# Attention written in pairs of beats: transposes of one, scores and projections of both, sums of one, transposes and sums of the other

## The chip, the cores and the metric

The kernel runs on one core of a Trainium2 chip. The metric is the device time of one execution in microseconds, from repeated runs; the changed kernel is compared with this one on the same chip. One execution was profiled; all rows here are from it.

## What is computed

One inference step of a trunk of two layers on 1024 latent tokens (a request in progress) and 256 context tokens, width 1024. The first layer mixes with two recurrences (mLSTM and SSD), the second with two attentions; each is followed by a squared-ReLU MLP, with RMSNorm and modulation around it. The change lies in the second layer's attentions:

```python
def odd_mixer_lat(h, k_ctx, v_ctx, ckv_ctx, kpe_ctx, cos_c, sin_c, cos_d, sin_d,
                  w_in, sink, q_a_norm, kv_a_norm, w_q_b, w_kv_b, w_out):
    ...
    oc = banded_attention(qc.reshape(Bsz, T, NKV_C, G_C, HD_C), kc, vc, k_ctx, v_ctx,
                          sink.reshape(NKV_C, G_C), HD_C ** -0.5)
    ...
    k, v = mla_keys_values(jnp.concatenate([ckv_ctx, ckv], axis=1),
                           jnp.concatenate([kpe_ctx, kpe], axis=1), w_kv_b)
    od = blocked_attention(qd[:, :, :, None], k, v, None, MLA_SCALE)
    return jnp.concatenate([oc.reshape(Bsz, T, -1), od.reshape(Bsz, T, -1)], axis=-1) @ w_out
```

`banded_attention` is grouped attention: 8 query heads, 2 key heads of 64, a band of 128 keys to either side, 256 context keys and a sink logit. `blocked_attention` on latent keys has 8 heads of 96 with all 1280 keys. The context tokens go through the same two without band, with 256 keys. All is in float32, and the kernel carries most products as three products of high and low parts.

## The kernel before

`Odd.run` issues the second layer's first projections, then the two attentions, and meanwhile the projections that the latent attention needs. All attention is cut into items that go through `weave` (line 2031):

- `Gqa` (line 1809): one tile of 128 queries and one key head with its four query heads; 10 tiles by 2, 20 items. Tiles 1 to 6 have five blocks of keys, three near and two of context; tiles 0 and 7 have four, and the context tokens' tiles 8 and 9 two.
- `Mla` (line 1919): two tiles of 128 latent queries and one head; 8 heads by 4, 32 items, five blocks of 256 keys each. The context tokens' share of a head is not an item; `Mla.alone` gives it in three steps.

The work goes in beats `n`. Every five beats an item starts, and its age `d` is the number of beats since. By age an item does this:

- `scores` at d = 0 to 4: products of queries and keys into PSUM. k = 0 and 1 fill the first score buffer (tag `S`, two buffers), k = 3 and 4 the second, k = 2 a third tile (tag `S3`, one buffer: `S3` in `Gqa`, `SB` in `Mla`). `Gqa` adds the band's mask by products with `idb`.
- `peak` at 1, 2 and 4: maxima on VectorE; `exps` at 3 to 6: exponentials on ScalarE from PSUM to SBUF (`Pm`, `Pmm`), with the sum in a second record, ACTIVATION_READ_ACCUMULATOR. In `Mla` exps at 3 and 5 read 1024 columns of `SA`, at 4 and 6 256 of `SB`; in `Gqa` each reads 512 of `S` and 128 of `S3`.
- `flip` at 7 and on, one for each block: four transposes of 128x128 by TensorE into a PSUM tile (`ptp`, `ptm`; tag `tp`, two buffers). `keep` in the same beat copies it to SBUF (`PT`, `PTm`), on VectorE at d = 9 and 11, on ScalarE else.
- `mix` one beat later: the product of block and values, summed in one PSUM bank (`po`, `pom`; tag `po`, one buffer). Values have 64 columns, so two such products stand in two halves of the array.
- `close` with the last mix, d = 12 with five blocks: the row sums' reciprocals (`R`, `Rm`, spread by POOL) are turned by products with the identity, ScalarE copies the sum, VectorE multiplies, and the bank is free again.

After the items' own work a beat calls `fill(n)`, which in beats 1, 2 and 4 of five takes one step of the extra projections: in the grouped stage the rest of the query projection (`qaps`, 8 pieces), the latent values (`vps`, 12), the queries' rotated parts (`qrps`, 10); in the latent stage `Mla.alone` (with scores `SC`, 8 times), and the next head's `qnps` (12), `knps` (24) and `qrtp` (transposes). Each lands in a tile with tag `tp` and is evicted by ScalarE and VectorE.

TensorE, ScalarE and VectorE run all of this in the order written:

```python
IN_ORDER = {mybir.EngineType.PE, mybir.EngineType.Activation, mybir.EngineType.DVE}
...
                with self.tc.manual_schedule(engines=IN_ORDER):
                    weave(nc, items(), fill)
```

A new tile in a buffer waits until the old tile's last reader is done; that is the only thing that holds an engine besides its data.

Of the kernel before, what the change touches and what calls it, by code (L numbers as in the profile page):

```python
# [75 lines left out]
KEEP = ((9,11),(9,11))  # L76
# [1732 lines left out]
class Gqa:  # L1809
# [31 lines left out]
    def scores(self, k):  # L1841
        if k == 2:
            if self.third:
                self.S3 = self.pp.tile([P, 4, P], F32, tag="S3", name="S3", bufs=1)
                for j in range(4):
                    self.product(self.S3[:, j], j, self.third[0], 1)
            return
        h = k - k // 3
        p, j = h // 2, h % 2
        if j == 0:  # L1850
            self.S[p] = self.pp.tile([P, 2, 512], F32, tag="S", name="S", bufs=2)
        for o, c0, nb in self.runs:
            self.product(self.S[p][:, j, o:o + nb * P], h, c0, nb)
# [176 lines left out]

def weave(nc, items, fill):

    act, dve = nc.scalar.copy, nc.vector.tensor_copy
    live, n = [], 0
    items = iter(items)
    while True:
        if n % 5 == 0:
            it = next(items, None)
            if it is not None:
                live.append((n, it))  # L2040
        live = [(b, x) for b, x in live if n - b <= 12]
        if not live:
            break
        at = [(n - b, x) for b, x in live]
        for d, x in at:
            if 0 <= d - 7 < x.tiles:
                x.flip(d - 7)
        for d, x in at:
            if d < 5:
                x.scores(d)  # L2050
        for d, x in at:
            if 0 <= d - 7 < x.tiles:
                x.keep(d - 7, dve if d in KEEP[0 if x.tiles < 5 or isinstance(x, Gqa) else 1] else act)
        for d, x in at:
            if d == SUMS:
                x.sums()
        for d, x in at:
            if d in (1, 2, 4):
                x.peak(d)
        for d, x in at:  # L2060
            if 3 <= d < 7:
                x.exps(d - 3)
        for d, x in at:
            if 0 <= d - 8 < x.tiles:
                x.mix(d - 8)
            if d - 8 == x.tiles - 1:
                x.close()
        fill(n)
        n += 1


KV_ORDER = (0, 1, 2, 3, 8, 9, 4, 5, 6, 7)
# [2 lines left out]
class Odd:  # L2075
# [332 lines left out]
    def run(self, late):  # L2408
        nc, net, a = self.nc, self.net, self.a
        pool = net.pool  # L2410
        with pool("od", 1) as cp:
# [113 lines left out]
            with pool("om", 4) as self.Pm, pool("oa") as sp, pool("oap", psum=True) as pp:  # L2525
# [41 lines left out]
                with self.tc.manual_schedule(engines=IN_ORDER):  # L2567
                    weave(nc, items(), fill)
                    while rest:
                        advance()  # L2570
# [54 lines left out]
```

## Time and profile before

| what | value |
| --- | --- |
| median of 3 runs | 3383.02 us (3382.25 to 3388.16) |
| the profiled execution | 3388.01 us, span of its instructions 3386.2 us |
| TensorE busy | 3233.2 us, 95% of the span |
| VectorE, ScalarE, POOL busy | 2250.5, 1634.0, 535.9 us |
| mean granted clock of TensorE | 0.980 |

The span runs from the first to the last instruction; the time has about 1.8 us more around it. A busy share is the union of the records of an engine. TensorE's matmuls are pipelined, and the end of a record is modelled: what two matmuls cost is the distance of their starts. The attention items run from about 1874 to 2457 us of the span.

### The profile page before, as it was taken

How to read it: one execution, taken by the hardware profiler on the slowest of the kernel's cores; microseconds unless marked ns; L12 is line 12 of the kernel's file. 1: busy time of each engine (PE TensorE's matmuls, PEld its weight loads, DVE VectorE, ACT ScalarE, POOL GpSimd, SP SyncE). 2: the span in 40 equal slices, each digit the busy share in tenths (PEclk: the TensorE clock that was granted, in tenths of full speed). 3: DMA queues.
4: the chain of work that ended last, by engine and by line, in shares of the span. 5: the costliest groups of instructions: out<-in, count | busy, mean ns of one | idle time of the engine just before them, and what ended most of it. 6: DMA issues, size and time to landing. Idle time of an engine off the chain costs nothing. (4 is left out here: it accounts for less than half of the span.)

```text
span 3386.2 us, 49959 instructions
## 1 busy us (share of the span) xinstructions
PE 3233.2 (95%) x17957; PEld 2644.1 (78%) x17957; DVE 2250.5 (66%) x4196; ACT 1634.0 (48%) x3827; POOL 535.9 (16%) x949
## 2 busy tenths in 40 slices
PE   7899999979999999999989999999999999999998
PEld 4898788858888888888787776666688788888887
DVE  4665866664598987788664466666746866556666
ACT  4444544453544444434563556555645444444443
POOL 1112222221111111001220240000011111110112
PEclk8999999979999999999999999999999999999999
DMA  7244343364355556565522210000233543365444
GB/s 216 71 110 116 104 140 102 81 203 142 115 171 179 182 181 227 181 204 159 160 95 90 72 40 26 9 5 7 83 132 108 175 143 142 119 208 171 156 142 174
DMA packets 319333, 435.26 MB, mean 129 GB/s; under 512 B 29772, under 2 KB 210348, under 8 KB 319084
## 3 DMA queue, kind: packets, MB, share of 16 engines
q1 hardware_dynamic: 296492, 343.17, 33.0%
q0 software_dynamic: 22592, 88.89, 7.0%
q8 instruction: 141, 2.31, 0.3%
q14 instruction: 108, 0.88, 0.1%
HBM read 309.55 MB, written 122.43 MB: 128 GB/s over the span
## 5 line engine op out<-in xcount | busy, mean ns | idle before, releaser
L194 PE MATMUL y<-oph 128*128 128x512 f32 x896 | 348.7, 389 | 1.7 <-DVE y L726 1.7
L196 PE MATMUL y<-oph,opl 128*128 128x512 f32 x896 | 348.6, 389 | 0.0
L195 PE MATMUL y<-opl,oph 128*128 128x512 f32 x896 | 348.6, 389 | 0.0
L200 DVE TENSOR_TENSOR opl<-sa,oph 128x512 fp32r<-128x512 f32 x216 | 158.9, 735 | 169.1 <-ACT oph L199 168.8
L199 ACT CAST oph<-sa 128x512 fp32r<-128x512 f32 x216 | 133.9, 620 | 263.9 <-PE y L195 180.2
L194 PEld LDWEIGHTS y<-oph 128*128 128x128 f32 x896 | 168.2, 188 | 37.1 <-DVE y L726 2.1
L195 PEld LDWEIGHTS y<-opl,oph 128*128 128x128 f32 x896 | 168.2, 188 | 35.1
L196 PEld LDWEIGHTS y<-oph,opl 128*128 128x128 f32 x896 | 168.2, 188 | 34.9
L480 POOL DMA_DIRECT2D hd<-x x96 | 52.0, 542 | 650.6 <-ACT x L482 507.0
L194 PE MATMUL mmf<-hh,wf_hi 128*128 128x512 f32 (+1 forms) x384 | 152.4, 397 | 0.0
L194 PE MATMUL mmt<-wt_hi,hh 128*128 128x256 f32 x480 | 148.0, 308 | 0.0
L196 PE MATMUL mmf<-hh,wf_lo 128*128 128x512 f32 (+1 forms) x384 | 139.3, 363 | 0.0
L195 PE MATMUL mmf<-hl,wf_hi 128*128 128x512 f32 (+1 forms) x384 | 138.9, 362 | 0.0
L195 PE MATMUL mmt<-wt_lo,hh 128*128 128x256 f32 x480 | 136.1, 283 | 0.0
L196 PE MATMUL mmt<-wt_hi,hl 128*128 128x256 f32 x480 | 136.0, 283 | 0.0
L1073 DVE SCALAR_TENSOR_TENSOR u<-pre,cw,u 128x510 f32<-128x510 f32 (+2 forms) x192 | 127.9, 677 | 7.2 <-ACT u L1071 6.3
L194 PE MATMUL o<-wh,hh 128*128 128x512 f32 x280 | 113.0, 404 | 0.0
L406 ACT ACTIVATE x<-x 128x512 f32<-128x512 f32 x112 | 70.2, 629 | 86.3 <-DVE x L640 65.7
L205 POOL TENSOR_SCALAR rs_v<-ss 128x1 f32<-128x1 f32 x85 | 30.5, 359 | 508.0 <-ACT junk L964 342.7
L196 PE MATMUL o<-wh,hl 128*128 128x512 f32 x280 | 110.5, 395 | 0.0
L195 PE MATMUL o<-wl,hh 128*128 128x512 f32 x280 | 110.1, 393 | 0.0
L2001 PE MATMUL pom<-PTm,mla_h 128*64 128x256 f32 x336 | 106.5, 402 | 2.4 <-DVE ob L2013 1.7
(1076 smaller groups left out, 10186.5 us busy)
## 6 DMA issues: line engine op xcount, KB each, us to landing
sa<-hd SPq DMA_DIRECT2D x108, 512.0 KB
hd<-s POOLq DMA_DIRECT2D x128, 320.0 KB, 3.0
hd<-x POOLq DMA_DIRECT2D x96, 320.0 KB, 2.6
wh<-in_w_down SPq DMA_DIRECT2D x40, 512.0 KB
wl<-in_w_down SPq DMA_DIRECT2D x40, 512.0 KB
w_raw<-in_w_ada SPq DMA_DIRECT2D x32, 512.0 KB
wh<-in_w_up SPq DMA_DIRECT2D x30, 512.0 KB
wl<-in_w_up SPq DMA_DIRECT2D x30, 512.0 KB
```

Source lines behind the costliest of these rows:

```text
L194: mm(ps, lh, rh, start=first and j == 0, stop=False)
L195: mm(ps, lh, rl, start=False, stop=False)
L196: mm(ps, ll, rh, start=False, stop=last and j == n - 1)
L199: self.nc.scalar.copy(hi, raw)
L200: self.nc.vector.tensor_tensor(lo, raw, hi.bitcast(F32), ALU.subtract)
L205: nc.gpsimd.tensor_scalar(v, ss, scale, eps, ALU.mult, ALU.add)
L406: relu = lambda o, i: nc.scalar.activation(o, i, AF.Relu)
L480: store = lambda i, z: nc.gpsimd.dma_start(hd[p, i], z)
L1073: nc.vector.scalar_tensor_tensor(us, pre[:, i:i + e - a], cw[:, b, j + i:j + i + 1], us, ALU.mult, ALU.add)
L2001: self.nc.tensor.matmul(self.po[64 * b:64 * b + 64, 0], self.odd.Vm[(0 if self.big else 10) + 2 * i + b][:, 64 * self.h:64 * self.h + 64], ...
```

## The change

`weave` takes two beats at a time. The steps of a beat become functions over the list of (age, item) of that beat, and a pair is written as: transposes, scores, copies and rows (sums, peaks, exponentials) of the first beat; scores of the second; both calls of `fill`; sums of the first; transposes, copies, rows and sums of the second. Nothing is added or left out.

```diff
--- before.py
+++ after.py
@@ -2030,27 +2030,27 @@
 
 def weave(nc, items, fill):
 
+
     act, dve = nc.scalar.copy, nc.vector.tensor_copy
     live, n = [], 0
     items = iter(items)
-    while True:
-        if n % 5 == 0:
-            it = next(items, None)
-            if it is not None:
-                live.append((n, it))
-        live = [(b, x) for b, x in live if n - b <= 12]
-        if not live:
-            break
-        at = [(n - b, x) for b, x in live]
+
+    def flips(at):
         for d, x in at:
             if 0 <= d - 7 < x.tiles:
                 x.flip(d - 7)
+
+    def keeps(at):
+        for d, x in at:
+            if 0 <= d - 7 < x.tiles:
+                x.keep(d - 7, dve if d in KEEP[0 if x.tiles < 5 or isinstance(x, Gqa) else 1] else act)
+
+    def scores(at):
         for d, x in at:
             if d < 5:
                 x.scores(d)
-        for d, x in at:
-            if 0 <= d - 7 < x.tiles:
-                x.keep(d - 7, dve if d in KEEP[0 if x.tiles < 5 or isinstance(x, Gqa) else 1] else act)
+
+    def rows(at):
         for d, x in at:
             if d == SUMS:
                 x.sums()
@@ -2060,13 +2060,39 @@
         for d, x in at:
             if 3 <= d < 7:
                 x.exps(d - 3)
+
+    def mixes(at):
         for d, x in at:
             if 0 <= d - 8 < x.tiles:
                 x.mix(d - 8)
             if d - 8 == x.tiles - 1:
                 x.close()
+
+    while True:
+        beats = []
+        for q in (n, n + 1):
+            if q % 5 == 0:
+                it = next(items, None)
+                if it is not None:
+                    live.append((q, it))
+            beats.append([(q - b, x) for b, x in live if q - b <= 12])
+        if not any(beats):
+            break
+        one, two = beats
+        flips(one)
+        scores(one)
+        keeps(one)
+        rows(one)
+        scores(two)
         fill(n)
-        n += 1
+        fill(n + 1)
+        mixes(one)
+        flips(two)
+        keeps(two)
+        rows(two)
+        mixes(two)
+        live = [(b, x) for b, x in live if n + 1 - b <= 11]
+        n += 2
 
 
 KV_ORDER = (0, 1, 2, 3, 8, 9, 4, 5, 6, 7)
```

What this does to TensorE's queue, at three places (numbers in names are buffers). The first is in the latent stage, where one item closes (`pom<-ident,Rm`) and the next begins its sum in the same bank; `qrtp` is a piece of projections. Before:

```order
L2007 MATMUL pom<-ident,Rm 64x128 x2
L2368 MATMUL qrtp<-ident,mla_l_19553 64x128
L2368 MATMUL qrtp<-ident,mla_l_19555 64x128
L2368 MATMUL qrtp<-ident,mla_l_19557 64x128
L2368 MATMUL qrtp<-ident,mla_l_19559 64x128
L1990 MATMUL ptm<-ident,Pmm 128x128 x4
L1938 MATMUL SA<-mhKA,moKB 128x512
L1939 MATMUL SA<-mhKA,moKB 128x512
L1940 MATMUL SA<-kpeT,mhVg 128x512
L2001 MATMUL pom<-PTm,mla_h_19564 64x256
L2001 MATMUL pom<-PTm,mla_l_19565 64x256
```

After:

```order
L2001 MATMUL pom<-PTm,mla_h_19548 64x256
L2001 MATMUL pom<-PTm,mla_l_19549 64x256
L2007 MATMUL pom<-ident,Rm 64x128 x2
L1990 MATMUL ptm<-ident,Pmm 128x128 x4
L2001 MATMUL pom<-PTm,mla_h_19540 64x256
L2001 MATMUL pom<-PTm,mla_l_19541 64x256
```

The projections and the score group (`SA`) no longer stand between closing and the next sum; four transposes do.

The second is a little later in the latent stage: the next item's third score tile `SB`, whose buffer the item before it read. Before:

```order
L1990 MATMUL ptm<-ident,Pmm 128x128 x4
L1938 MATMUL SA<-mhKA,moKB 128x512
L1939 MATMUL SA<-mhKA,moKB 128x512
L1940 MATMUL SA<-kpeT,mhVg 128x512
L2001 MATMUL pom<-PTm,mla_h_19570 64x256
L2001 MATMUL pom<-PTm,mla_l_19571 64x256
L1990 MATMUL ptm<-ident,Pmm 128x128 x4
L1938 MATMUL SB<-mhKA,moKB 128x256
```

After:

```order
L2001 MATMUL pom<-PTm,mla_h_19544 64x256
L2001 MATMUL pom<-PTm,mla_l_19545 64x256
L1990 MATMUL ptm<-ident,Pmm 128x128 x4
L1938 MATMUL SA<-mhKA,moKB 128x512
L1939 MATMUL SA<-mhKA,moKB 128x512
L1940 MATMUL SA<-kpeT,mhVg 128x512
L1938 MATMUL SB<-mhKA,moKB 128x256
```

A sum and a transposes block stood ahead of `SB`; now it follows the score group `SA` at once, and the pair before ends with a sum and transposes.

The third is in the grouped stage: the last scores of one item (the first `S` rows) and the first of the next one (the last row). Before:

```order
L1834 MATMUL S<-KA,Qg 128x256
L1838 LDWEIGHTS idb
L1838 MATMUL S<-mq,idb 128x128
L1839 MATMUL S<-KB,Qg 128x256
L1834 MATMUL S<-KA,Qg 128x256
L1839 MATMUL S<-KB,Qg 128x256
L1905 MATMUL po<-PT,Vg 64x256 x2
L194 MATMUL vps<-kbv_19576,ckT_17328 128x512
L195 MATMUL vps<-kbv_19577,ckT_17328 128x512
L196 MATMUL vps<-kbv_19576,ckT_17329 128x512
L1895 MATMUL ptp<-ident,Pm 128x128 x4
L1834 MATMUL S<-KA,Qg 128x256
```

After:

```order
L1895 MATMUL ptp<-ident,Pm 128x128 x4
L1834 MATMUL S<-KA,Qg 128x256
L1838 LDWEIGHTS idb
L1838 MATMUL S<-mq,idb 128x128
L1839 MATMUL S<-KB,Qg 128x256
L1834 MATMUL S<-KA,Qg 128x256
L1839 MATMUL S<-KB,Qg 128x256
L1834 MATMUL S<-KA,Qg 128x256
```

A sum, a piece of projections (`vps`) and transposes lay between the two; nothing does now.

## Rows read from the trace of the kernel before

**Rows 1.** Windows: length, busy PE, PEld, DVE, ACT, POOL, clock, DMA.

```profile
1874.00:2457.00 583.00, 571.14 (x3816) 394.44 (x3816) 375.02 (x748) 343.40 (x902) 73.22 (x155) 1.00 0.11 34
```

**Rows 2.** Timeline of TensorE, latent stage: start, us, engine, line, operation.

```profile
2190.09 0.38 PE L2001 MATMUL pom<-PTm,mla_h 128*64 128x256 f32 x1
...
2190.40 0.66 PE L1990 MATMUL ptm<-ident,Pmm 128*128 128x128 f32 x4
2190.82 0.48 PE L1938 MATMUL SA<-mhKA,moKB 128*128 128x512 f32 x1
2191.13 0.40 PE L1939 MATMUL SA<-mhKA,moKB 128*128 128x512 f32 x1
2191.37 0.40 PE L1940 MATMUL SA<-kpeT,mhVg 128*128 128x512 f32 x1
2191.69 0.43 PE L2001 MATMUL pom<-PTm,mla_h 128*64 128x256 f32 x1
...
2191.96 0.38 PE L2001 MATMUL pom<-PTm,mla_h 128*64 128x256 f32 x1
...
2192.28 0.51 PE L194 MATMUL knps<-ckT,mla_h 128*128 128x512 f32 x1
2192.62 0.40 PE L195 MATMUL knps<-ckT,mla_h 128*128 128x512 f32 x1
2192.86 0.40 PE L196 MATMUL knps<-ckT,mla_l 128*128 128x512 f32 x1
2193.09 0.38 PE L1990 MATMUL ptm<-ident,Pmm 128*128 128x128 f32 x2
```

**Rows 3.** Timeline of a close, latent stage, all engines.

```profile
2180.42 0.60 PE L2007 MATMUL pom<-ident,Rm 128*64 128x128 f32 x4
...
2180.95 0.66 PE L1990 MATMUL ptm<-ident,Pmm 128*128 128x128 f32 x4
2181.06 0.37 ACT L2009 COPY mt<-pom 64x256 f32<-64x256 f32 x1 [1.95 <-PE pom L2007]
...
2181.46 0.41 DVE L2010 TENSOR_TENSOR mt<-mt,pom 64x256 f32<-64x256 f32 x1 [0.37 <-ACT mt L2009]
...
2181.70 0.59 ACT L1994 COPY PTm<-ptm 128x512 f32<-128x512 f32 x1 [0.28 <-PE ptm L1990]
2181.91 0.41 DVE L2013 TENSOR_TENSOR ob<-mt,pom 64x256 f32<-64x256 f32 x1
...
2182.18 1.12 ACT L1976 ACTIVATE Pmm<-SA,nmm 128x1024 f32<-128x1024 f32 x1
...
2183.28 0.48 ACT L1976 ACTIVATE Pmm<-SB,nmm 128x256 f32<-128x256 f32 x1
...
2183.64 0.21 ACT L1976 ACTIVATION_READ_ACCUMULATOR Pmm<-SB,nmm 128x1 f32 x1
```

**Rows 4.** Timeline of ScalarE, grouped stage.

```profile
1924.02 0.58 ACT L1899 COPY PT<-ptp 128x512 f32<-128x512 f32 x1
1924.48 0.71 ACT L1876 ACTIVATE Pm<-S,nm 128x512 f32<-128x512 f32 x1
...
1925.16 0.38 ACT L1878 ACTIVATE Pm<-S,nm 128x128 f32<-128x128 f32 x1
...
1925.50 0.71 ACT L1876 ACTIVATE Pm<-S,nm 128x512 f32<-128x512 f32 x1
```

**Rows 5.** Timeline of TensorE, grouped stage: a score group and the next sum.

```profile
1921.68 0.36 PE L1834 MATMUL S<-KA,Qg 128*128 128x256 f32 x1
...
1922.45 0.44 PE L1905 MATMUL po<-PT,Vg 128*64 128x256 f32 x2
```

**Rows 6.** Timeline of the small requests' scores, latent stage.

```profile
2124.10 0.28 PE L1940 MATMUL SC<-kpeT,moVg 128*128 128x256 f32 x1
...
2124.43 0.69 DVE L2018 TENSOR_REDUCE mxm<-SC 128x2 f32<-128x512 f32 x1 [0.27 <-PE SC L1940]
...
2125.90 0.46 ACT L1976 ACTIVATE Pma<-SC,nmm 128x256 f32<-128x256 f32 x1
```

## The prediction

> **What bounds it now.** Three views, in this order. First the page's shares by engine: TensorE leads, so the question is what stands between its matmuls. Second the busy time of the attention stage alone, which is all that the change touches: of 583 us TensorE's records cover 571.1 at a granted clock of 1.00, VectorE's 375 and ScalarE's 343 [rows 1]. So TensorE sets the pace there, hardly waits (583 - 571.1 = 11.9 us), and the other two have slack as sums, though not at every point. Third the timeline of a few beats, for two things: how far apart TensorE's starts are from kind to kind, and how long the chains on ScalarE and VectorE are that give its buffers back.
>
> The starts [rows 2]: four transposes take 0.42 us (2190.40 to the first score at 2190.82, the reader sees four in one row). A latent score group of three takes 0.31 + 0.24 = 0.55 to its last start, and 0.32 from there to the first sum, so 0.08 more than the 0.24 within the group. A sum block is 0.27 (2191.69 to 2191.96) and then 0.31 to the next transposes (2190.09 to 2190.40). With a piece of extra projection between, the last sum start to the next transposes is 1.13 (2191.96 to 2193.09), so the piece costs 0.82, though three such products in a row have starts only 0.24 apart, 0.71 together: 0.32 and 0.34 are paid at its entry.
>
> **What is removed.** Per pair of beats the order was twice transposes, scores, sums, projections; now it is transposes, scores, scores, projections, sums, transposes, sums. Number and shape of all instructions stay. Without projections nothing is saved: two entries into sums and two exits remain, and a score group behind transposes costs no more than one behind scores (0.42 + 0.31 against four pitches of 0.11 and 0.24, within 0.05). Transposes followed by a sum do not occur in these rows; by the nearest, score to sum, I price them at 0.08 over the transposes' own pitch, and at zero and 0.10 as bounds, which moves nothing below by more than 0.02. With a projection piece, it now follows scores of its own kind, and 0.82 falls to 0.71: 0.11 saved. The loops issue 12 + 10 + 8 such pieces in the grouped stage and 12 + 24 + 8 in the latent stage, 74 in all: **-8 us**. The Trainium skill, TensorEngine Tiling (Array Packing), section Key Properties, says that a change of the array's tiling mode drains the engine. Sums write 64 columns and all else 128, so it would count four mode changes in a pair before and four after, and save nothing here. The rows have an extra 0.10 on the second projection start, behind the mode change, so they and not the rule are used; by the rule the sum below would be 8 us higher (a rival).
>
> TensorE's present waits may go too, between 0 and all 11.9 us. I take **-4**, a third: the transposes that wait for a projection's eviction keep their two buffers, the wait of the small requests' transposes does not stay.
>
> **What is added: waits.** A buffer must come back before TensorE may overwrite it, and ScalarE works in written order. Items start every five beats, so every second one (call it A) starts in the first beat of a pair; its successor B starts in a second beat. What was a full beat between A's last reader and B's first writer is now much less. Four places, time from a row each.
>
> *Output bank of the latent stage.* A closes at d=12, in a first beat; B's first sum follows one transposes block later (the first order piece). From the closing matmuls' start to the end of the last multiply is 1.90 us (2180.42 to 2181.91 + 0.41 [rows 3]): copy on ScalarE, add and multiply on VectorE. TensorE needs 0.53 to the next transposes, 0.42 for these and 0.08: 1.03. Wait 0.87. Before, a score group (0.87) was between as well: 1.82 of cover against 1.90, or 2.64 with a projection. 16 times: **+13.9**. Queued behind are all of TensorE's later work and thus both other engines.
>
> *Third score tile of the latent stage.* SB has one buffer. A reads it last in exps at d=6 (first beat); B writes it at d=7 (second beat), and only B's scores of one group and no sum are now between that beat's transposes and the write (second order piece). Count from the transposes at d=5, in the second beat before: the copy starts at 0.75 (2180.95 to 2181.70), the 1024-wide exponential at 1.23, the 256-wide at 2.33, its accumulator read ends at 2.90 [rows 3]. TensorE: transposes and entry 0.50, sums 0.58, transposes 0.42, score group 0.79: it is there at 2.29. Wait 0.61 (0.52 if the read need not end). Before, another 0.87 + 0.58 and a transposes block lay between: 4.16, cover of 1.26. 16 times: **+9.8**.
>
> *Score banks of the grouped stage.* Same pattern twice. B's k=0 at d=5 needs A's exps(1) of d=4 (third order piece); B's k=2 at d=7 needs A's exps(3) of d=6. From the transposes: copy at 0.75, first exps 0.46 later, second 1.02 later, at 2.23 [rows 4]. The bank is read until 2.94. TensorE comes at 0.50 + 0.58 + 0.42 + 0.69 = 2.19 (a grouped score group is 0.77 up to the next sum, less 0.08 [rows 5]). Wait 0.75. For k=2 the last reader is the 128-wide exponential, 0.68 later and 0.38 long: until 3.29, wait 1.10. Rivals inside: 0.85 and 1.2 with the accumulator reads. The output bank's wait here lies within the first. Taken 0.8 and 1.15 for the six tiles with a third block: 11.7; two tiles without, about 0.5 each by the shorter exps: **+12.7**.
>
> *Small requests.* SC takes a transposes buffer. In pairs the next pair's first transposes get that buffer; before, they got the other one. Its reduction starts 0.33 after the last SC start, the second exponential ends 1.93 after the reduction's start [rows 6]: 2.26. TensorE needs 0.20 (half of 0.24, plus 0.08) + 0.58 + 0.50 + 0.58 = 1.86. Wait 0.4 to 0.5 (with the read); 8 heads: **+3.6**. These exponentials now also stand ahead of the d=6 one in ScalarE's queue; the same wait covers that.
>
> Evictions of projections have cover elsewhere: in a pair with one piece, sums, transposes and sums (1.66) stand against a copy of 0.59 (the shape of the copy in [rows 3]) and a VectorE pass like it. Two pieces in a pair have less (a rival). POOL's and SP's queues keep their order but for a few neighbours; what POOL copies for a closing step has some four beats of lead.
>
> **Sum.** 13.9 + 9.8 + 12.7 + 3.6 = 40.0, less 8 and 4: +28. The profiled execution took 3388.0 (span 3386.2 plus 1.8 around), 5 above the median of the runs shown, 3383.0. Set on the median: 3411.
>
> **Rivals.**
> *Projections save nothing* (0.07): the entry cost is one of leaving the sums and is paid again where transposes now follow them twice in a pair; then -8 falls away, 3419. For it: 0.31 stands behind a sum whatever follows. Against: the 0.34 behind it has no like behind transposes, whose pitch is 0.11 at once. This is what the Trainium skill's drain at a mode change (TensorEngine Tiling (Array Packing), Key Properties) would make of it.
> *Half the waits* (0.13): the chains are shorter, since ScalarE starts the exponentials before the copy's record ends and a bank is free at the read, not at the signal; 20 - 12 = +8, 3391. For it: the exponential starts 0.48 into a 0.59 copy [rows 3]. Against: that is in the sums already.
> *More waits* (0.11): pairs with two pieces (of beats 1, 2 and 4 in five; two fall together once in ten beats) make the second transposes wait for the first piece's eviction behind SB's wait; 0.4 each, 26 times: +10, 3421.
> *Faster* (0.08): one mechanism, projections among scores. If all 11.9 us of idling go with the regrouping and entry costs are saved as counted, 20 us come back; it decides where the four waits come to less than 20, half of mine. With a third of them, 13: 3376. Against: the waits need only a strict queue order, and the chains' rows have no loose end that long.
> *No difference* (0.06): waits and savings cancel, 3383, or ScalarE's exps were not queued where I think.
> *As summed* (0.55): 3411.
>
> The range goes from the half-wait case's end, 3390, to 3430: all four at their upper ends (43) with hardly any saving. A change within 0.2%, 7 us, can't be told from none here: below 3376 faster, above 3390 slower. Faster 0.08, same 0.08 (no difference and a little of the half case), slower 0.84.
>
> **What would show it.** Right: in the waits by engine, TensorE's sum (pom) behind VectorE's ob with some 14 us and waits of 0.9; SB behind ScalarE's Pmm with 10; S in the grouped stage behind Pm with 11 or more; the attention stage some 28 us longer with the same busy time, all else equal. The projections' second start at 0.24 instead of 0.34. Wrong: SB starting right behind SA, or ob's wait under 0.4; transposes followed by sums costing much more than 0.08; or a stage other than attention changing.

## The result, and the profile after

The changed kernel takes 3436.69 us (median of 4 runs, 3432.59 to 3452.31) against 3384.53 us (4 runs): a ratio of 1.016, 95% interval 1.0144 to 1.0176. It is slower, as forecast, but by 52 us, not by 28.

The profiled execution took 3452.31 us, the longest of the four, so what is read from it is some 15 us longer than the median run. The view by windows of TensorE (length, busy time, instructions, granted clock as a share of 2.4 GHz, DMA share, GB/s), first the attention of the changed kernel from its first score to its last sum, then stretches of it:

```profile
1867.55:2522.33 654.78, 597.71 (x3906) 0.98 0.10 32
...
1867.00:1880.00 13.00, 11.27 (x73) 0.79 0.24 85
1880.00:1928.00 48.00, 44.91 (x339) 0.96 0.14 42
1928.00:1978.00 50.00, 40.46 (x277) 0.93 0.27 82
1978.00:2112.00 134.00, 124.54 (x886) 1.00 0.12 34
2112.00:2492.00 380.00, 350.88 (x2179) 1.00 0.04 12
2492.00:2523.00 31.00, 26.86 (x164) 0.94 0.42 145
```

The same view of the kernel before, from its first score to its last sum:

```profile
1861.32:2455.44 594.12, 581.34 (x3905) 1.00 0.11 35
```

Attention is 60.7 us longer: TensorE's idle time rose by 44.3 us (12.8 to 57.1) and its busy time by 16.4. Outside of it the span is 3.6 us longer (64.3 in all). That need be no effect of the change: the first score starts 6.2 us later in this run, with the same code ahead of it, and at 1856.7, 1855.7 and 1860.2 us in the profiled runs of e4, e6 and e16 below. The longest waits of TensorE within the attention, by engine and line waited for (us in total, times, longest):

```profile
PE pom L2001 <- DVE ob L2013: 14.9, 16, 1.3
PE S L1834 <- ACT Pm L1876: 10.0, 5, 6.5
PE SB L1938 <- ACT Pmm L1976: 7.7, 16, 1.3
PE S L1834 <- ACT Pm L1878: 5.9, 6, 1.4
PE ptp L1895 <- ACT Pm L1876: 3.2, 3, 2.2
PE po L1905 <- DVE og L1914: 2.9, 6, 0.5
...
PE ptp L1895 <- DVE mhKB L2378: 2.0, 2, 1.3
PE ptm L1990 <- DVE moKB L2378: 1.7, 2, 0.8
PE pom L2001 <- DVE PTm L1994: 1.5, 2, 1.3
```

The reader sees three of the four places that the prediction names: the output bank (ob) 16 times, the third score tile (SB) 16 times, and the score banks of the grouped stage, in its third block (Pm L1878) six times and in its first (Pm L1876, with the sums behind og). The fourth, the small requests, is not there: no transposes of TensorE wait for Pma (the small requests' exponentials), where the kernel before had two such waits (1.6 us). One entry was not foreseen: a single wait of 6.5 us.

The output bank, in the timeline of the changed kernel, to be laid beside [rows 3]:

```profile
2166.58 0.60 PE L2007 MATMUL pom<-ident,Rm 128*64 128x128 f32 x4
2167.11 0.66 PE L1990 MATMUL ptm<-ident,Pmm 128*128 128x128 f32 x4
2167.22 0.37 ACT L2009 COPY mt<-pom 64x256 f32<-64x256 f32 x1 [2.45 <-PE pom L2007]
2167.62 0.41 DVE L2010 TENSOR_TENSOR mt<-mt,pom 64x256 f32<-64x256 f32 x1 [0.72 <-ACT mt L2009]
...
2168.07 0.41 DVE L2013 TENSOR_TENSOR ob<-mt,pom 64x256 f32<-64x256 f32 x1
...
2168.62 0.40 PE L2001 MATMUL pom<-PTm,mla_h 128*64 128x256 f32 x1 [0.85 <-DVE ob L2013]
```

From the closing matmuls (2166.58) to the end of the multiply is 1.90 us, just the chain of [rows 3]; TensorE has 0.53 and a transposes block to cover it and stands for 0.85. The third score tile:

```profile
2150.18 1.12 ACT L1976 ACTIVATE Pmm<-SA,nmm 128x1024 f32<-128x1024 f32 x1
...
2151.01 0.39 PE L1940 MATMUL SA<-kpeT,mhVg 128*128 128x512 f32 x1
...
2151.29 0.47 ACT L1976 ACTIVATE Pmm<-SB,nmm 128x256 f32<-128x256 f32 x1
...
2151.64 0.21 ACT L1976 ACTIVATION_READ_ACCUMULATOR Pmm<-SB,nmm 128x1 f32 x1
2151.90 0.39 PE L1938 MATMUL SB<-mhKA,mhKB 128*128 128x256 f32 x1 [0.51 <-ACT Pmm L1976]
```

SB starts 0.89 after the last start of the SA group, where 0.24 is the usual distance: 0.65 late, and it starts with the end of the accumulator read. The forecast had 0.61.

A projection piece behind scores (the second and third product of it, to be laid beside the piece in [rows 2]):

```profile
2188.66 0.40 PE L194 MATMUL knps<-ckT,mla_h 128*128 128x512 f32 x1
2188.89 0.40 PE L195 MATMUL knps<-ckT,mla_h 128*128 128x512 f32 x1
2189.13 0.40 PE L196 MATMUL knps<-ckT,mla_l 128*128 128x512 f32 x1
2189.46 0.43 PE L2001 MATMUL pom<-PTm,mla_h 128*64 128x256 f32 x1
```

The second start follows at 0.23, not at 0.34. That saving is there, and not in this piece alone: from the last score start to the first sum start with a `knps` piece between is 1.02 us (median of 15), less 0.32 without a piece 0.70. Before, from sums to transposes, it was 1.12 (median of 15), less 0.31 without a piece 0.81.

Last, the single wait. ScalarE in the changed kernel:

```profile
1947.79 0.21 ACT L1878 ACTIVATION_READ_ACCUMULATOR Pm<-S,nm 128x1 f32 x1
1954.99 0.62 ACT L2310 CAST kbv<-kb_raw 128x512 fp32r<-128x512 f32 x1 [6.99 <-DMA kb_raw<-in_w_kv_b]
1955.52 0.68 ACT L1876 ACTIVATE Pm<-S,nm 128x512 f32<-128x512 f32 x1
```

The copy of the weights for the latent stage waits 7 us for its load, and the exponentials that free TensorE's score banks stand behind it in the queue. SyncE issued the load at 1947.90, behind a store of the item that had just closed (`mixo<-og`, 1946.75), and ScalarE was at the copy 0.1 us later. In the kernel before, SyncE issued the load at 1931.29, ahead of such a store (1932.05), and ScalarE was at the copy 3.0 us later and waited 1.6. What TensorE's clock does there, by windows of 5 us:

```profile
1945.00:1950.00 5.00, 4.83 (x37) 1.00 0.58 157
1950.00:1955.00 5.00, 0.00 (x0) 0.94 0.81 262
1955.00:1960.00 5.00, 3.66 (x13) 0.50 0.03 7
1960.00:1965.00 5.00, 5.00 (x36) 0.88 0.53 140
1965.00:1970.00 5.00, 4.41 (x31) 1.00 0.60 201
```

In the window in which it starts again it is granted 0.50, the lower of its two levels (1.2 GHz), in the next 0.88, and in the third full speed.

### The profile page after: what moved, and what is told of

Read it like the earlier page. It is cut to its first block, busy times and chain, and to the rows that moved or that the text cites. A ratio compares the mean times of both kernels' runs of the same rounds, so it can differ in the third digit from the quotient of the medians.

```text
span 3450.5 us, 49954 instructions
## 1 busy us (share of the span) xinstructions
PE 3246.3 (94%) x17957; PEld 2651.7 (77%) x17957; DVE 2245.0 (65%) x4196; ACT 1642.4 (48%) x3827; POOL 538.5 (16%) x949
## 5 line engine op out<-in xcount | busy, mean ns | idle before, releaser
L195 PEld LDWEIGHTS y<-opl,oph 128*128 128x128 f32 x896 | 168.2, 188 | 34.9
L2001 PE MATMUL pom<-PTm,mla_h 128*64 128x256 f32 x336 | 108.2, 404 | 16.4 <-DVE ob L2013 14.9
L1990 PEld LDWEIGHTS ptm<-ident,Pmm 128*128 128x128 f32 x640 | 67.4, 141 | 63.7 <-issue 35.9
L1990 PE MATMUL ptm<-ident,Pmm 128*128 128x128 f32 x640 | 105.4, 287 | 6.9 <-DVE moKB L2378 1.7
```

Source lines behind the costliest of these rows:

```text
L195: mm(ps, lh, rl, start=False, stop=False)
L1990: self.nc.tensor.transpose(self.pt[:, (2 * b + j) * P:(2 * b + j + 1) * P], self.Pm[j][:, (2 * i + b) * P:(2 * i + b + 1) * P], self.ident)
L2001: self.nc.tensor.matmul(self.po[64 * b:64 * b + 64, 0], self.odd.Vm[(0 if self.big else 10) + 2 * i + b][:, 64 * self.h:64 * self.h + 64], ...
```

## Experiments

Ratios are to the kernel before on the same chip, with 95% intervals; the changed kernel's own is 1.016 (1.0144 to 1.0176). One thousandth is 3.4 us.

**Which part of the order costs.** e2 calls `fill` behind the sums again, e3 writes the second scores behind the first sums:

```diff
         scores(two)
-        fill(n)
-        fill(n + 1)
         mixes(one)
+        fill(n)
         flips(two)
...
         mixes(two)
+        fill(n + 1)
```

```diff
-        scores(two)
         fill(n)
         fill(n + 1)
         mixes(one)
+        scores(two)
         flips(two)
```

Expected of e2_projections_back:

> The changed kernel with each piece of projections again behind the sums of its own beat; the scores of both beats stay together. Theory (buffers that come back late, the chains as counted): a closing step in a first beat is now followed by a piece of projections (0.8 us) before the transposes, so the wait of TensorE's next sum for VectorE's ob falls from 0.93 to about 0.1 (-14 us), the waits of SB for ScalarE stay at 0.6 (10 us), waits for evictions of projections mostly go (-5), the wait for the weights' load shrinks (-3), and the 7 us saved on projections are paid again: -15, some 3422 us. Rival (TensorE loses by the sequence of kinds, transposes and sums twice in a pair): that sequence stays, 3437 and the entry cost on top, 3444.

Expected of e3_scores_apart:

> The changed kernel with the second beat's scores behind the first beat's sums; both pieces of projections stay ahead of them. Theory (late buffers): SB, S and S3 get a sum and the projections as cover and do not wait (-10 in the latent stage, -14 in the grouped one), the output bank gets a score group as cover (0.93 to about 0.2, -11), the second transposes wait less for evictions (-4); the one long wait for the weights' load stays: -39, some 3398 us. Rival (sequence of kinds): one more change between kinds in a pair, so no gain, 3437 or slower.

Measured: e2 1.0121 (1.0101 to 1.0141), e3 1.0039 (1.0023 to 1.0056). Against the changed kernel that is 13 and 41 us less, where 15 and 39 were expected. Of the loss of 16 thousandths 12, some 41 us, come with the scores of both beats standing together; in e3's trace the output bank's wait is 6.3 us instead of 14.9 (4.8 in e2's), and the rows of SB and of Pm L1878 are gone.

**ScalarE's queue.** e4 gives one more of five copies to VectorE (`KEEP = ((9,10,11),(9,10,11))`).

Expected of e4_copies_on_vector:

> The changed kernel with the copy of transposes at age 10 on VectorE instead of ScalarE (one item of two has it ahead of the 1024-wide exponential that SB waits for). Theory (ScalarE's chain of copy and two exponentials holds SB and S3): SB's wait falls from 0.6 to 0.1 (-8), S3's in the grouped stage from 1.1 to about 0.6 (-3), the wait for ob stays at 15 us, VectorE gets 0.1 us more work per copy: -11, some 3426 us. Rival (SB waits for its maximum on VectorE, or for something else than this queue): no gain or a loss, 3437 to 3445.

Measured 1.0123 (1.0103 to 1.0143): 12 to 13 us less. The waits of TensorE in its attention:

```profile
PE pom L2001 <- DVE ob L2013: 15.4, 16, 1.3
...
PE SB L1938 <- ACT Pmm L1976: 1.3, 1, 1.3
...
PE S L1834 <- ACT Pm L1878: 0.2, 1, 0.2
```

SB's wait fell from 7.7 to 1.3 and Pm L1878's from 5.9 to 0.2, together 12.1, and the output bank's stayed. So these two waits are set by what stands in ScalarE's queue, as the prediction counted them, and they are worth what they show.

e7 issues the last exponential of an item with the third, a beat earlier (`if 3 <= d < 6: x.exps(d - 3)`, and `if d == 5: x.exps(3)`).

Expected of e7_third_exps_early:

> Changed kernel, with the last exponential of an item issued a beat earlier, behind the third one, so that the third score tile (SB, S3) is given back a beat earlier. The theory has this exponential as the last reader that SB waits for (16 times 0.6 us) and as the one that the third score block of the grouped stage waits for (six times 1.1): both waits go, 10 + 6 us, 3421. The rival has ScalarE's queue as the limit, so that the longer row of exponentials in that beat delays the copies of the transposes behind it, and TensorE waits for those instead: 3434 to 3440.

Measured 1.0164 (1.0149 to 1.0179), and SB's row reads 7.6, 16 as before: neither the gain nor the loss that was expected came. In the timeline of SB above, the two exponentials already run back to back, with no copy between them on ScalarE, and so they do in e7: their order in the queue is the same, and the edit is no test of who holds SB. It is the start of the row that counts, which e4 moves.

**The closing step.** e6 lets VectorE copy the lower half of the output bank and does the add and the multiply from SBUF:

```diff
-        tmp = self.sp.tile([64, 2, P], F32, tag="og", name="mt", bufs=2)
-        nc.scalar.copy(tmp, po[64:128, 0])
-        nc.vector.tensor_tensor(tmp, tmp, po[0:64, 0], ALU.add)
         r = 64 * (self.h % 2)
+        low = self.sp.tile([P, 2, 2, P], F32, tag="og", name="low", bufs=2)[r:r + 64]
         dst = self.ob[r:r + 64, self.t * P:(self.t + 2) * P].rearrange("p (j t) -> p j t", j=2)
-        nc.vector.tensor_tensor(dst, tmp, po[0:64, 1], ALU.mult)
+        nc.scalar.copy(dst, po[64:128, 0])
+        nc.vector.tensor_copy(low, po[0:64])
+        nc.vector.tensor_tensor(dst, dst, low[:, 0], ALU.add)
+        nc.vector.tensor_tensor(dst, dst, low[:, 1], ALU.mult)
```

Expected of e6_short_close:

> Changed kernel, with another closing step in the latent stage: ScalarE copies the upper half of the output bank while VectorE copies the lower half, and the add and the multiply then read SBUF, so that the bank is free after one pass instead of three; one VectorE copy more for each tile. If the bank's wait is set by this chain, as predicted, TensorE's wait of 0.93 us for VectorE before the sums (14.9 us over 16 tiles) falls to 0.1 to 0.3, and the time by about 11 us, to 3426. The rival has the closing step late because evictions of projections stand ahead of it in both queues: then only the 0.4 us of the last pass go, at most 6 us, 3431. If other waits take its place: 3437.

Measured 1.0151 (1.0136 to 1.0166). The wait fell to 10.6 us only. Its timeline:

```profile
2153.13 0.60 PE L2007 MATMUL pom<-ident,Rm 128*64 128x128 f32 x4
...
2153.76 0.37 ACT L2011 COPY ob<-pom 64x256 f32<-64x256 f32 x1 [2.45 <-PE pom L2007]
2154.16 0.68 DVE L2012 COPY low<-pom 64x512 f32<-64x512 f32 x1 [0.72 <-ACT ob L2011]
...
2154.90 0.43 PE L2001 MATMUL pom<-PTm,mla_h 128*64 128x256 f32 x1 [0.59 <-DVE low L2012]
```

The two copies of one bank did not overlap: VectorE waits for ScalarE's to end. The chain became 0.27 us shorter (2.04 to 1.77 from the closing matmuls to the next sum), 15 times 0.27 is 4, about what went from the wait (14.9 to 10.6). The time fell by 3 us, within the intervals, where 11 were expected: the bank is not free after one pass.

e5 is the kernel before, single beats, with `fill(n)` ahead of the sums; e8 is e5 with the sums ahead of `fill(n)` in beats that close an item (here the edit of e8 against the kernel before):

```diff
+        ends = any(d - 8 == x.tiles - 1 for d, x in at)
+        if not ends:
+            fill(n)
         for d, x in at:
             if 0 <= d - 8 < x.tiles:
                 x.mix(d - 8)
             if d - 8 == x.tiles - 1:
                 x.close()
-        fill(n)
+        if ends:
+            fill(n)
         n += 1
```

Expected of e5_projections_before_sums:

> The kernel before, beat by beat, with the piece of projections ahead of the beat's sums and nothing else changed. Theory (entry cost of a piece is saved where it follows scores, 0.10 us for 74 pieces, and no buffer comes back later): -7, some 3377 us, and no wait over 0.3 for ob or SB. Rival (the saving is taken back, because the piece's eviction or the closing step now has less cover): 3384 or slower.

Expected of e8_closing_first:

> The single-beat order with projections ahead of the sums (e5_projections_before_sums), except that in beats which close an item the sums and the closing step go first. In e5 the sums waited 10.7 us for the output bank (28 times), and its timeline has the closing copy and add queued behind the evictions of the projection: the theory expects this wait to fall to 2 us or less, and 7 to 9 us less time than e5, 1.005 of before. The rival, that the bank is late by its own chain of three passes whatever stands ahead, leaves e5's 1.0074.

Measured: e5 1.0074 (1.0053 to 1.0094), a miss by some 32 us: a saving of 7 was expected and a loss of 25 came. e8 1.0017 (1.0006 to 1.0027), 19 us less than e5, more than twice the 7 to 9 expected. The closing step in e5's timeline shows why:

```profile
2156.59 1.17 ACT L2350 CAST moKB<-qnps 64x512 fp32r<-64x512 f32 x2 [1.75 <-PE qnps L196]
...
2156.97 0.60 PE L2007 MATMUL pom<-ident,Rm 128*64 128x128 f32 x4
...
2157.78 0.37 ACT L2009 COPY mt<-pom 64x256 f32<-64x256 f32 x1
2157.79 1.39 DVE L2352 TENSOR_TENSOR moKB<-qnps,moKB 64x512 fp32r<-64x512 f32 x2 [0.78 <-ACT moKB L2350]
...
2159.22 0.41 DVE L2010 TENSOR_TENSOR mt<-mt,pom 64x256 f32<-64x256 f32 x1
2159.66 0.41 DVE L2013 TENSOR_TENSOR ob<-mt,pom 64x256 f32<-64x256 f32 x1
...
2160.22 0.40 PE L2001 MATMUL pom<-PTm,mla_h 128*64 128x256 f32 x1 [1.36 <-DVE ob L2013]
```

The projection's eviction (moKB) was issued ahead of the closing copy and add, so they stand behind it on both engines, and the bank comes back 3.1 us after the closing matmuls instead of 1.9. An item with five blocks closes in the beats whose number leaves 2 when divided by five, and in those `fill` takes a step. In e8 the output bank's wait is 1.8 us (10.7 in e5), and the transposes' wait behind Pma 1.4 (6.0 in e5): 13.5 of the 19.

e16 does the same in the changed kernel (`mixes(one)` ahead of both `fill` where it closes an item).

Expected of e16_pairs_closing_first:

> The changed kernel, except that in a pair whose first beat closes an item its sums and closing step go ahead of the projections. The pieces then lie between the closing step and the next item's first sums, and no eviction stands ahead of the closing copy and add. The theory expects the output bank's wait (14.9 us) to fall to about 5 and the time by 8 us, 1.0135 of before. The rival, that the second transposes then wait for the evictions of those pieces instead, has 1.015 to 1.016.

Measured 1.0165 (1.0151 to 1.0179): nothing. The output bank's wait did fall to 4.8 us, but S behind Pm L1876 rose from 10.0 to 12.7, new waits came (SA 1.8, sums behind smm 1.7), and transposes wait 1.9 behind moVg: the time is the rival's. The pieces of those pairs also stand behind sums again.

**The load and the pieces.** e1 has one more step ahead of the copies that read the load (`SPLA = (0,3,3,3,2)`), e10 has none in the kernel before (`(0,3,3,3,0)`), and e9 writes `fill(n + 1)` ahead of `mixes(two)`.

Expected of e1_load_lead:

> One number of the changed kernel is altered: one more step of the extra work lies between the load of kb_raw and the copies that read it. My theory has a one-off of 6.8 us in the changed kernel (ScalarE stands 7.0 us at the copy into kbv, waiting for that load, and the exponentials queued behind it hold back TensorE's scores at 1956 us): it expects that wait to fall under 2 us and the time to fall by 4 to 7 us, to 3430 to 3433. The rival has the load hidden in any case, because TensorE would wait for other things there: 3437, no change.

Expected of e10_before_no_lead:

> The kernel before with one number altered: no step of the extra work lies between the load of kb_raw and the copies that read it. If the load's one-off in the changed kernel is the lost lead and nothing else, this kernel shows the same wait here: ScalarE 5 to 7 us at kbv (1.6 before), TensorE's scores behind it 3 to 6 us late, granted clock under 1.00 in the 20 us behind the stall, and 5 to 9 us more time (1.0015 to 1.003). The rival, that the wait belongs to the order of the beats and the old order has work to cover it, has 1.000.

Expected of e9_pieces_apart:

> Changed kernel, but the projection pieces of the second beat stand ahead of the second sums instead of with those of the first beat. The theory has some 10 us of the time in transposes that wait for the evictions of two pieces that fall in one pair, and a part of the load's one-off of 6.8 us in the same neighbourhood; and a piece behind the second transposes also covers the output bank's wait where it falls. It expects a gain of 10 to 15 us, 3422 to 3427. The rival has the neighbourhood of two pieces worth nothing, and the waits for banks as the whole loss: then only the cover counts, and at most 5 us go, 3432 to 3437.

Measured: e1 1.0148 (1.0132 to 1.0163), e10 1.0003 (0.9995 to 1.0012), e9 1.0157 (1.0138 to 1.0177). In e1 ScalarE's wait for the load fell from 7.0 to 2.3 us and the 6.5 us of TensorE vanished, but the next transposes now wait 2.5 us: 4 us at most, and the intervals of the two kernels overlap. In e10 ScalarE waits 3.9 us, TensorE 2.7, and no time is lost that could be measured: the old order has cover, as the rival said. In e9 two pieces no longer meet, the wait of 6.5 us is gone (S behind Pm L1876 is 3.4 in all), and the time is the same: the waits only change their names (transposes behind Pma 4.7 us, vps 2.8, qnps 2.1).

**What was left of e3 and e8.** Both still had one long stall in the grouped stage. VectorE in e8:

```profile
1932.84 1.22 DVE L1860 TENSOR_REDUCE mx<-S 128x2 f32<-128x1024 f32 x1
1934.09 6.61 DVE L1866 TENSOR_TENSOR mx<-mx 128x2 f32<-128x2 f32 x1
1940.73 0.16 DVE L1867 SCALAR_TENSOR_TENSOR nm<-mx,sinkn 128x2 f32<-128x2 f32 x1
```

and GpSimd in e8, in the same time:

```profile
1933.71 0.75 POOL L2288 CAST mla_h<-kb_raw 128x256 fp32r<-128x256 f32 x2
...
1939.42 1.25 POOL L2289 TENSOR_TENSOR mla_l<-qb_raw,mla_h 128x512 fp32r<-128x512 f32 x1
```

An instruction on 128x2 elements, 0.16 us elsewhere, lasts 6.61 us and ends as GpSimd's row of splits ends (1939.42 + 1.25). TensorE waits 5.2 us for what is behind it. e11 (from e3) and e12 (from e8) put the copies of the splits on ScalarE (`SPLA = (0,2,2,3,1)`), e13 (from e8) shifts the splits by a step (`(0,3,3,3,2)`), and e14 leaves the grouped stage as before and has e8's order in the latent stage alone (`ends = n < 100 or any(...)`).

Expected of e11_scores_apart_scalar_splits:

> The changed kernel with the second scores apart again (e3_scores_apart, 1.0039 of before), with the copies of the weight splits on ScalarE instead of GpSimd. In e3 one VectorE instruction on 128x2 elements, 0.16 us elsewhere, lasted 5.22 us while GpSimd worked through these splits without a gap, TensorE waited 3.7 us for it, and its granted clock over the 40 us around was 0.79. The theory: with GpSimd's row broken by waits for ScalarE, that instruction stays under 1.5 us, the 3.7 us and most of the 8 us of lost clock go, 1.0005 to 1.002. The rival: the copies now stand in ScalarE's queue ahead of exponentials and cost as much, 1.003 to 1.005.

Expected of e12_closing_first_scalar_splits:

> e8_closing_first with the copies of the weight splits on ScalarE. In e5 one VectorE instruction on 128x2 elements lasted 6.60 us beside GpSimd's splits and TensorE waited 5.2 us behind it, with a granted clock of 0.80 over those 40 us. With both causes gone the saving at the entry of the projections (6 us by e5's rows) should be left over: 0.999 to 1.002. The rival, that projections ahead of the sums cost by themselves, has 1.004 or more.

Expected of e13_closing_first_lead:

> e8_closing_first (single beats, projections ahead of the sums but for closing beats, 1.0017 of before) with one more step of extra work ahead of the weight splits. In e8 one VectorE instruction on 128x2 elements lasted 6.61 us beside GpSimd's splits, TensorE waited 5.2 us, and its granted clock was 0.86 over 50 us: 9 of the 6.7 us that its attention is longer than before's lie there, so all else gains. If the step moves the instruction out of GpSimd's unbroken row, that cost goes: 0.998 to 0.9995. If it meets the row again: 1.001 to 1.003.

Expected of e14_latent_closing_first:

> The kernel before with projections ahead of the sums in the latent stage alone, but for beats that close an item; the grouped stage is as before. In e8 the latent stage (first SA to last pom) was 373.5 us against 376.0 before. Theory (a piece behind scores saves its entry cost, 0.11 us, in those beats): 2 to 3 us less, 0.999 to 0.9995. Rival (the saving is given back by the evictions): 1.000 or more.

Measured: e11 1.0052 (1.004 to 1.0064), e12 1.0017 (1.0005 to 1.0029), e13 1.0014 (1.0003 to 1.0025), e14 0.999 (0.998 to 1.0). In none of the first three is the stall gone: VectorE's instruction still lasts 2.88, 4.35 and 6.61 us. In e11 and e12 the copies of the splits bring a wait of their own into ScalarE's queue, for the load of qb_raw (4.5 us in two waits in e11, 7.2 in one in e12), and TensorE waits 6.9 and 7.6 us behind it. So e11 comes out at its rival, e12 inside the expected range but not by the expected road, and e13 as it said for an instruction that meets the row again. e14 does what was expected of it: the latent stage takes 373.5 us (first SA to last pom) against 376.0, and the kernel is some 3 us faster than before, the best of all that ran, at the edge of what can be told (the interval reaches 1.0).

e17 joins e16, e4 and e1.

Expected of e17_pairs_three_undone:

> The changed kernel with three things at once: the closing step ahead of the projections (e16), one more copy of each five on VectorE (e4, 9 us less), and one more step of lead for kb_raw (e1, 4 us less). If the causes are separate the gains add up: 8 + 9 + 4 = 21 us, 1.0098 of before (1.0085 to 1.011). If they are one and the same slack, it stops near 1.012.

Measured 1.0099 (1.0083 to 1.0115), 21 us back. The sum came as expected, though e16 by itself gave nothing. What the three gave one by one, 16 us, lies inside the intervals too (13 to 28 us back), so e17 does not tell whether the gains add up; e4's 12 us are the one part that is shown by itself.

## Why the prediction came out as it did

3437 lies above the end of the range, 3430. Direction and main mechanism were right; the range let only the four waits of the sum grow ("all four at their upper ends"), and what it left out is below.

**The mechanism.** Buffers come back later than TensorE wants them, at three of the four places named, since half of the items start in a second beat. Forecast of the waits: 40.0 us. The rows after: 14.9 + 7.7 + 5.9 + 2.9, and 3.5 of the 10.0 behind Pm L1876 (10.0 less the one of 6.5), 34.9 of idle time. A wait's idle time begins only when the last record ends, so a start is later than its idle time says: 0.65 against 0.51 for the SB shown. With some 0.15 for each of the 48 such waits it is some 42. That this is so near to 40.0 is in part luck: by place, with the 0.15, the output bank has 17 (13.9 forecast), SB 10 (9.8) and the grouped stage 15 (12.7), while the small requests' 3.6 did not come. e3 takes most of these waits away and e4 a part, in the amounts shown.

**The saving was right.** -8 for 74 pieces, 0.11 for each; the `knps` pieces show 0.11, and e14 has 2.5 of the 3.2 us that two thirds of the latent stage's 44 pieces would give.

**What failed**, in the prediction's own steps:

1. *"TensorE's present waits may go too ... I take -4."* Some went, but others of more weight came. What is left of the idle time, 57.1 - 34.9 - 6.5, is 15.7 us where the kernel before had 12.8 in all. *"Evictions of projections have cover elsewhere"* is the sentence behind it: transposes wait for them eight times behind a pair with two pieces (4.7 us in all) and twice, for mhKB, behind a pair with one (2.0). The rival *More waits* had the first, with +10 and a chance of 0.11. It should have been a term, of half that size. e5 shows the same thing at its largest: work that is issued ahead of a closing step is ahead of it in every queue.
2. *"POOL's and SP's queues keep their order but for a few neighbours."* One neighbour counted: SyncE has a store ahead of the load where it had it behind, and the distance from the load's issue to its use fell from 3.0 us to 0.1. The load's 6.5 us on TensorE are in no term. By e1 more lead wins back some 4 of them, hardly more than can be told, and in e9 the wait went without any gain.
3. *"The attention stage some 28 us longer with the same busy time, all else equal"*: [rows 1] had a clock of 1.00, and it was carried over. It fell in the windows shown. Length times what is missing to 1.00 gives 2.7 + 1.9 + 3.5 + 1.9 = 10 us in the profiled run. That is an upper bound, since it counts idle time too. Part of this need be no effect of the change: at the start, where e7, e9 and the changed kernel hardly differ, the first 12 us were granted 0.99, 0.86 and 0.80. The 0.93 in the 50 us around the load comes back in e4, e16 and e17. Over all runs of a kernel the mean of this measure (1 less the granted clock, times the time) is 69.7 us for the changed kernel (4 runs) and 62.0 for the one before (29 runs beside e8), so some 8 us; but the longest run alone has 83, and by medians it is 67 against 64, so 3. Nor was the busy time the same: it rose by 16.4, of which the saving (-8), the clock (10) and the ends of records ahead of the 48 waits (7) make 9.

28, with 2 for the waits, 7 for the first point (from -4 to +3), 4 to 6.5 for the second and 3 to 8 for the third, makes some 44 to 51 of the 52; the rest stays open. The pieces are read from rows, and no run held the clock apart from the stalls, so their split is argued, not shown; e1, e6, e9 and e16 say that waits here stand in for one another, so that they can't be undone one by one.

The clock bears on one more thing. e8, e12 and e13 have each 68 to 69 us by that measure, 6 to 7 more than before, and are 4 to 6 us slower by their means; less that measure their means are 3323.3, 3323.7 and 3322.6 us, and before's 3324.0 and 3324.9. So what they lose is of the size of the lower clock behind their one stall, as in this window of e8, with 1.00 in the same place of e14; the stall itself and the saving on projections would then about cancel. This is argued from sums, not shown:

```profile
1919.48:1969.48 50.00, 43.14 (x276) 0.86 0.30 92
```

**Rivals.** *Half the waits*, *Faster* and *No difference* fall with the waits above, *Projections save nothing* with the `knps` pieces.

## What to carry to other kernels

When steps are regrouped, count for each buffer what stands between its last reader and its next writer, and do the same for each load and its first use, and for each eviction that would now be issued ahead of a step that frees a bank: what is issued earlier is ahead in every engine's queue. A stall of TensorE can have a second price, the clock behind it (0.50 and 0.88 in the two windows behind the 6.5 us here), which a sum of waits leaves out. Keep work that closes an item ahead of work that can wait: that was worth 19 us in single beats (e8 against e5), though nothing in pairs (e16), where other waits took its place.

## What the hardware showed that was not expected

- A VectorE instruction of two SBUF inputs on 128x2 elements lasted 5.22 us in e3, 6.60 in e5, 6.61 in e8 and e13 and 4.35 in e12 beside an unbroken row of GpSimd instructions, 0.16 in the median of each run, and ended with the row each time; with half of the row moved to ScalarE (e11, e12) it was shorter and still ended with the row. The Trainium skill, SBUF — State Buffer, section Who interferes with whom, says that such an instruction contends with a GpSimd instruction that reads SBUF, that the lock on the shared ports is exclusive and that the order of issue decides who blocks. The traces agree that the one that came second is blocked, but here the block lasted for the rest of a row of up to some ten instructions, not for one of them (0.4 to 1.4 us). In other places (1.19 us in e6, 1.01 in e2) the same instruction came through between two GpSimd instructions that stood back to back; what decides between the two stays open.
- Two copies of one output bank, by ScalarE and by VectorE, ran one after the other (e6: 2153.76 + 0.37, then 2154.16). The trace has VectorE waiting for ScalarE's semaphore, so the program ordered them; that the hardware would not have let them overlap is not shown.
- The granted clock was 0.50 in the window of 5 us behind a stall of 6.5 us, 0.88 in the next and 1.00 in the third. Of the changed kernel's four runs (3452.3, 3437.8, 3435.6 and 3432.6 us at 0.976, 0.981, 0.982 and 0.980) the longest has the lowest mean clock; the other three show no order.
